# Gate and up products as seven products of halves per feature tile, and a down projection in three chunks whose input is read back from DRAM

## The chip, the cores and the metric

The kernel runs on one core of one Trainium2 chip. The metric is the device time of one execution in microseconds (us), from the first instruction to the last. The core has five engines with a queue of instructions each: TensorE (PE in the profile; PEld are its weight loads), VectorE (DVE), ScalarE (ACT), GpSimd (POOL) and SyncE (SP), which here issues the DMA transfers. Each engine works through its own queue in order, and waits on semaphores for the others.

## The reference

One hybrid decoder layer with batch 1, 512 tokens, 2048 features and 5632 hidden features in the channel sub-layer, all in float32.

```
mod = silu(c) @ w_ada + b_ada
sh_m, sc_m, g_m, sh_f, sc_f, g_f = split(mod, 6)
h = modulate(rms_norm(x, norm_mix_g), sh_m, sc_m)
p = h @ w_in
...                      # RG-LRU heads and RWKV-7 heads over all tokens
x = x + g_m * (concat([y_a, y_b]) @ w_out)
h = modulate(rms_norm(x, norm_ffn_g), sh_f, sc_f)
gate, up = split(h @ w_gu, 2)
x = x + g_f * ((silu(gate) * up) @ w_down)
return rms_norm(x, final_norm_g)
```

Here `modulate(h, shift, scale)` is `h * (1 + scale) + shift`. The change is about the last three lines.

## The kernel before

**Layout.** Activations lie transposed: 128 features on the partitions, all 512 tokens along the free axis. A tile of features is one index `k` (16 tiles of the 2048 features) or `f` (44 tiles of the 5632 hidden ones). Weights are packed ahead of the launch so that one DMA brings the 128 output columns of one tile for a run of input features.

**Products.** A float32 product is made of three products in the format float32r. `split_into` (L105, L106) splits an operand exactly: ACT casts it to the high part, and DVE subtracts that part from the operand to get the low one. `mm3` (L124 to L126) then multiplies high by high, high by low and low by high. `load_split` issues the DMA of a weight piece into a raw tile (L115) and splits it, ahead of what else is queued on ACT and DVE if its data are there (`high_priority`). `gemm_steps` runs a whole product over its input tiles `k`; each step is three matmuls of 128x512, each with a weight load of its own.

**Order.** A scheduler takes the program in the order in which it is written and puts each instruction on its engine's queue; `high_priority` moves work ahead. In the mixing sub-layer `weave` orders several streams by estimated latencies; that part is left as it is. A tile pool has a fixed number of buffers per tag, and a new tile waits until the buffer's last reader is done.

**The channel sub-layer** is `channel` (L912 to L977). First the second half of the output projection (`project`) adds to the residual tiles `x1`, which stay in SBUF, and modulation columns 68 to 79 are made beside it (`mod_steps`, L198 and L199). Then comes the norm (`norm`), and `modulate` (L247, L251, L252) makes 16 pairs of high and low parts, `hhi` and `hlo`. Four chunks follow. Each chunk makes 11 hidden tiles: for each, a gate product and an up product of 16 steps of `k`, silu (L957), a product (L958) and a split into `shi` and `slo`, which stay in SBUF. Then the chunk multiplies its 11 tiles into all 16 output tiles and adds the result to `x1` (L969). The last modulation columns, 80 to 95, are made in the first chunk (L963 to L965). At the end come a norm and the stores of the output.

The raw weight tiles of this part hold 1024 columns (8 input tiles) and have two buffers, the split ones three (L939). The SBUF pool `big` has 32 buffers of one 128x512 tile. PSUM has eight banks under five tags, `mm` 2, `st` 1, `gr` 2, `ch` 2 and `y` 1; here `mm`, `st` and `gr` take turns.

## Time and profile before

| | |
|---|---|
| time, three runs | 2515.35, 2515.86 (median) and 2519.14 us |
| profiled execution, span | 2515.8 us, 30983 instructions; no other time is given for it |
| up to 914 us | mixing sub-layer and the first half of the output projection, PE busy 849.5 us |
| 914 to 1045 us | second half of the output projection and the norm, PE busy 120.2 of 131 us |
| 1045 to 2495 us | gate, up and down, PE busy 1440.8 of 1450 us, DVE 500.5, ACT 348.1, POOL none |
| 2495 to 2516 us | last norm and stores, PE busy 3.4 us |
| DMA | 333.22 MB in all, mean 132 GB/s |

A matmul's row in the profile is longer than the time until the next one starts, since matmuls overlap in the engine. A busy PE is thus read by counting matmuls over a stretch of time, not by the length of a row. In the lists of instruction groups, a line has the source line, the engine, the operation, output and inputs by the program's names, shapes and the count; then busy time and mean duration of one in ns; then the idle time ahead of them with what ended it. In a timeline, the first number is the start in us, and the second the duration.

### The profile page before, as it was taken

Reading aid. Unit: us, or ns where it says so; the run is one execution under the profiler, and the core shown is the slowest. Engines: PE = TensorE matmul, PEld = TensorE weight load, DVE = VectorE, ACT = ScalarE, POOL = GpSimd, SP = SyncE. Lnnn points to the kernel's source line nnn. Section 1 sums busy time; section 2 is a strip of 40 time slices with the busy share of each in tenths; the row PEclk is TensorE's granted clock in tenths of the full one; section 3 lists DMA queues with packets and bytes.
Section 4 is the critical chain, followed back from the end, with each engine's and each line's share of the span. In section 5 each row is a group of like instructions: output and inputs, shape, how many; then the busy total and the mean of one; then the engine's idle time right before and its main releaser. Section 6 shows DMA issues by size and latency. Waiting matters only on the chain.

```text
span 2515.8 us, 30983 instructions
## 1 busy us (share of the span) xinstructions
PE 2413.9 (96%) x11560; PEld 1953.4 (78%) x11560; DVE 1380.4 (55%) x3111; ACT 843.7 (34%) x1340; POOL 82.0 (3%) x131
## 2 busy tenths in 40 slices
PE   5999999999999999899999999999999999999997
PEld 3677777877777886687788888888888888888885
DVE  7979898999969847854423322233322233222244
ACT  4357364455355333432222222222222222222221
POOL 0000111111101000000000000000000000000000
PEclk9999998999999999999999999999999999999998
DMA  8864444444342438366423332323333233333233
GB/s 304 308 219 130 148 128 143 131 152 144 125 135 81 143 108 283 119 195 194 160 90 95 108 100 93 101 83 98 106 98 99 89 92 105 101 93 100 85 95 112
DMA packets 138938, 333.22 MB, mean 132 GB/s; under 512 B 15458, under 2 KB 28898, under 8 KB 134690
## 3 DMA queue, kind: packets, MB, share of 16 engines
q1 hardware_dynamic: 138788, 331.25, 40.7%
q8 instruction: 90, 1.47, 0.2%
q14 instruction: 60, 0.49, 0.1%
HBM read 322.92 MB, written 7.87 MB: 131 GB/s over the span
## 4 chain that ended last, share of the span: by engine, by line
PE 72%; DVE 9%; DMA 7%; issue 1%; ACT 1%; SPq 0%; POOL 0%; DVEq 0%; ACTq 0%
PE ps_mm L124 10%; PE ps_mm L126 10%; PE ps_mm L125 10%; PE ps_gr L126 6%; PE ps_st L124 6%; PE ps_gr L124 6%; PE ps_st L126 6%; PE ps_gr L125 6%; PE ps_st L125 6%; DMA adaq<-in_w_ada 6%; DVE adaq L199 2%; DVE wlo L106 2%; DVE rw_xp L764 1%; DVE rw_x L766 1%; DMA wraw<-in_w_out 1%
## 5 line engine op out<-in xcount | busy, mean ns | idle before, releaser
L106 DVE TENSOR_TENSOR wlo<-wraw,whi 128x1024 fp32r<-128x1024 f32 (+2 forms) x552 | 496.7, 902 | 730.2 <-ACT whi L105 721.1
L105 ACT CAST whi<-wraw 128x1024 fp32r<-128x1024 f32 (+2 forms) x552 | 436.6, 792 | 1292.4 <-PE ps_mm L125 401.1
L124 PE MATMUL ps_mm<-hhi,whi 128*128 128x512 f32 x1020 | 417.1, 410 | 9.8 <-ACT hhi L251 7.2
L126 PE MATMUL ps_mm<-hhi,wlo 128*128 128x512 f32 x1020 | 407.2, 399 | 1.7 <-DVE wlo L106 1.6
L125 PE MATMUL ps_mm<-hlo,whi 128*128 128x512 f32 x1020 | 406.5, 399 | 0.8 <-DVE hlo L252 0.7
L124 PEld LDWEIGHTS ps_mm<-hhi,whi 128*128 128x128 f32 x1020 | 193.4, 190 | 53.2 <-ACT hhi L251 9.9
L125 PEld LDWEIGHTS ps_mm<-hlo,whi 128*128 128x128 f32 x1020 | 193.7, 190 | 43.4 <-DVE hlo L252 4.8
L126 PEld LDWEIGHTS ps_mm<-hhi,wlo 128*128 128x128 f32 x1020 | 193.8, 190 | 42.3 <-DVE wlo L106 3.0
L199 DVE SCALAR_TENSOR_TENSOR adaq<-adaq,cbq 128x512 f32<-128x512 f32 x256 | 173.5, 687 | 92.9 <-DMA adaq<-in_w_ada 85.1
L126 PE MATMUL ps_gr<-hhi,wlo 128*128 128x512 f32 x496 | 193.7, 390 | 3.1 <-DVE wlo L106 3.1
L126 PE MATMUL ps_st<-hhi,wlo 128*128 128x512 f32 x496 | 193.6, 390 | 2.0 <-DVE wlo L106 2.0
L124 PE MATMUL ps_st<-hhi,whi 128*128 128x512 f32 x496 | 194.0, 391 | 1.6 <-ACT hhi L251 1.6
L125 PE MATMUL ps_gr<-hlo,whi 128*128 128x512 f32 x496 | 193.5, 390 | 0.0
L125 PE MATMUL ps_st<-hlo,whi 128*128 128x512 f32 x496 | 193.5, 390 | 0.0
L124 PE MATMUL ps_gr<-hhi,whi 128*128 128x512 f32 x496 | 192.6, 391 | 0.0
L126 PEld LDWEIGHTS ps_gr<-hhi,wlo 128*128 128x128 f32 x496 | 93.4, 188 | 23.6 <-DVE wlo L106 4.1
L126 PEld LDWEIGHTS ps_st<-hhi,wlo 128*128 128x128 f32 x496 | 93.4, 188 | 21.8 <-DVE wlo L106 2.5
L124 PEld LDWEIGHTS ps_st<-hhi,whi 128*128 128x128 f32 x496 | 93.5, 188 | 21.6 <-ACT hhi L251 2.2
L125 PEld LDWEIGHTS ps_gr<-hlo,whi 128*128 128x128 f32 x496 | 93.7, 189 | 19.6
L124 PEld LDWEIGHTS ps_gr<-hhi,whi 128*128 128x128 f32 x496 | 93.7, 189 | 19.4
L125 PEld LDWEIGHTS ps_st<-hlo,whi 128*128 128x128 f32 x496 | 93.3, 188 | 19.8 <-DVE hlo L252 0.3
L766 DVE TENSOR_TENSOR rw_x<-rw_x,rw_xp 128x27 f32<-128x27 f32 (+23 forms) x496 | 94.7, 196 | 5.7
(312 smaller groups left out, 3809.6 us busy)
## 6 DMA issues: line engine op xcount, KB each, us to landing
wraw<-in_w_gu SPq DMA_DIRECT2D x176, 512.0 KB, 3.6
adaq<-in_w_ada SPq DMA_DIRECT2D x256, 256.0 KB, 3.3
wraw<-in_w_in SPq DMA_DIRECT2D x160, 256.0 KB, 3.0
ada<-in_w_ada SPq DMA_DIRECT2D x32, 1024.0 KB, 7.2
wraw<-in_w_down SPq DMA_DIRECT2D x64, 512.0 KB, 3.5
wraw<-in_w_out SPq DMA_DIRECT2D x64, 256.0 KB, 3.3
wraw<-in_w_down SPq DMA_DIRECT2D x64, 192.0 KB, 2.3
x<-in_x SPq DMA_DIRECT2D x32, 256.0 KB, 5.3
```

The source lines that it names most:

```text
L105: nc.scalar.copy(out=hi, in_=src)
L106: nc.vector.tensor_tensor(out=lo, in0=src, in1=hi.bitcast(F32), op=ALU.subtract)
L124: mm(ps, lhsT=w[0], rhs=x[0], start=start, stop=False)
L125: mm(ps, lhsT=w[0], rhs=x[1], start=False, stop=False)
L126: self.pe = mm(ps, lhsT=w[1], rhs=x[0], start=False, stop=stop).ins
L199: nc.vector.scalar_tensor_tensor(out=t, in0=t, scalar=1.0, in1=cb, op0=ALU.mult, op1=ALU.mult, accum_out=part[:, m, h:h + 1])
L764: tt(out=pr[:, :n, :j], in0=at[:, s + 1:, s:s + 1].to_broadcast([P, n, j]), in1=x[:, s:s + 1, :j].to_broadcast([P, n, j]), op=ALU.mult)
L766: tt(out=x[:, s + 1:, :j], in0=x[:, s + 1:, :j], in1=pr[:, :n, :j], op=ALU.add)
```

## The change

The product of a gate tile and an up tile with the hidden input is now taken as a two by two block product. The tokens are halved (256 each), the input features are halved (1024 each), and the two columns of blocks are the gate tile and the up tile. Of the eight block products that this takes, the form of Strassen and Winograd needs seven, on sums and differences of blocks. `b11` and `b21` are the two halves of a gate tile's weights, `b12` and `b22` those of the up tile's.

`group` makes one gate tile and one up tile by seven products, in the order 1, 2, 6, 5, 7, 4, 3. Each has 8 steps of `k` with three matmuls of 128x256, into half a PSUM bank. The weight sums are made on the raw tiles ahead of their split: `b11 + b12` on POOL (L1139), plus `b22` on DVE into `t2` (L1141), `t2 + b21` on DVE (L1144) and `b12 + b22` on POOL (L1152). DVE takes the seven products out of PSUM (L1136 to L1162) and ACT one (L1133). `gu_end` (L1010) applies silu, multiplies and stores the hidden tile to DRAM.

The activations' side of each product is made once, by `operands` and `from_h`: it modulates halves of `x1` in place (L970, L972), POOL makes sums and differences of them (L994 to L996, L1007), and each is split into a tile `comb`. This is done beside the first two groups, which run in step; the other 42 follow one by one. The residual is stored to DRAM beforehand (`x1d`, L944), because `x1` is overwritten, and read again (`x1r`, L1046).

The down projection starts when all 44 hidden tiles are there. It has three chunks, of 15, 15 and 14 tiles, which are read from DRAM into `sraw` (two buffers) and split. A chunk's product for one output tile takes a piece of 1024 columns and one of 896 or 768. The 64 steps for the modulation columns 80 to 95 stand in groups 10 onward in the program, two a group; in DVE's queue they come in groups 2 to 12 (L199). The pool `big` has 8 buffers of four tiles (`quad_view`). The weight pool `wf` has ten raw buffers instead of two; it is opened at the start of `channel`, and its tiles of 1024 columns serve the second half of the output projection as well.

```diff
-        self.open_weights(ctx, "wf", 1024, 2, 3)
+        self.wmctx.close()
+        self.open_weights(ctx, "wf", 1024, 10, 3)
...
+            def done(m):
+                self.square(acc, xt[m], m, fp)
+                nc.sync.dma_start(out=self.x1d[m], in_=xt[m])
+            self.after_project = done
...
-        h = [self.modulate(xt[k], self.cols[:, 16 + k:17 + k], rstd, self.mod[:, 48 + k:49 + k],
-                           yp.tile([P, S], F32R, tag="h", name="hlo")) for k in range(KT)]
...
-                pg, pu = ps(), ps()
-                self.gemm(pg, i["w_gu"][2 * m], h)
-                self.gemm(pu, i["w_gu"][2 * m + 1], h)
-                t = fp.tile([P, S], F32, tag="ft", name="sil", bufs=2)
-                hi = fp.tile([P, S], F32R, tag="shi", name="shi", bufs=FC)
-                lo = fp.tile([P, S], F32R, tag="slo", name="slo", bufs=FC)
-                self.split_into(hi, lo, t)
-                s.append((hi, lo))
-            if cf == 0:
-                with self.tc.issue_after(last):
-                    self.mod_cols(range(80, 96), self.wm, ("raw", 3, "raw", 3))
...
-                self.gemm(p, i["w_down"][cf, m], s)
...
+        self.cp = gctx.enter_context(tc.tile_pool(name="cp", bufs=6))
+        self.ev = gctx.enter_context(tc.tile_pool(name="ev", bufs=2))
...
+        def modulate(q, side):
+            sl = slice(side * 256, side * 256 + 256)
+            for z in range(4):
+                k = 4 * q + z
+                v = quads[q][:, z, sl]
+                stt(out=v, in0=v, scalar=self.cols[:, 16 + k:17 + k], in1=rstd[:, sl],
+                    op0=ALU.mult, op1=ALU.mult)
+                nc.scalar.activation(out=v, in_=v, func=AF.Identity, bias=self.mod[:, 48 + k:49 + k])
...
+        def from_h(p):
+            if p == 1:
+                modulate(0, 0)
+                modulate(1, 0)
+                return [view(0, 0), view(1, 0)]
+            if p == 2:
+                modulate(2, 0)
+                modulate(3, 0)
+                return [view(2, 0), view(3, 0)]
+            if p == 6:
+                for j in range(2):
+                    modulate(j, 1)
+                    modulate(2 + j, 1)
+                    t = self.staging()
+                    pool_tt(out=t, in0=view(j, 1), in1=view(2 + j, 1), op=ALU.subtract)
+                    pool_tt(out=view(j, 1), in0=view(j, 0), in1=view(j, 1), op=ALU.subtract)
+                    pool_tt(out=view(j, 0), in0=t, in1=view(j, 0), op=ALU.subtract)
+                    s1.append(t)
+                return [view(0, 0), view(1, 0)]
+            if p == 5:
+                return s1
+            if p == 7:
+                return [view(0, 1), view(1, 1)]
+            if p == 4:
+                return [view(2, 1), view(3, 1)]
+            s4 = [self.staging(), self.staging()]
+            for j in range(2):
+                pool_tt(out=s4[j], in0=view(2 + j, 0), in1=view(j, 0), op=ALU.add)
+            return s4
+        def gu_end(m, g, u):
+            nc.scalar.activation(out=g, in_=g, func=AF.Silu)
+            nc.vector.tensor_tensor(out=g, in0=g, in1=u, op=ALU.mult)
+            nc.sync.dma_start(out=sd[m], in_=g)
...
+        mods = self.mod_steps(range(80, 96), fq, ("ft", 2, "x1", 2))
+        g0, g1 = self.group(stage, 0), self.group(stage, 1)
+        for p in order[:-1]:
+            self.operands(stage, p)
+            next(g0)
+            next(g1)
+        self.operands(stage, 3)
+        for g in (g0, g1):
+            for _ in g:
+                pass
+        for m in range(2, FT):
+            g = self.group(stage, m)
+            for p in order:
+                next(g, 0)
+                if m >= 10 and p in (6, 4):
+                    next(mods, 0)
...
+        xt = []
+        for k in range(KT):
+            xt.append(self.quad_view(k, "x1r", F32))
+            nc.sync.dma_start(out=xt[k], in_=self.x1d[k])
+        gctx.close()
+        for n in (15, 15, 14):
+            s = []
+            for f in range(base, base + n):
+                t = fq.tile([P, S], F32, tag="x1", name="sraw", bufs=2)
+                nc.sync.dma_start(out=t, in_=sd[f])
+                hi = sp.tile([P, S], F32R, tag="shi", name="shi", bufs=15)
+                lo = sp.tile([P, S], F32R, tag="slo", name="slo", bufs=15)
+                self.split_into(hi, lo, t)
+                s.append((hi, lo))
+            for m in range(KT):
+                p = self.ps(("mm", "gr", "ch")[m % 3])
+                self.gemm(p, i["w_down"][m][:, base * P:(base + n) * P], s)
+                stt(out=xt[m], in0=p, scalar=self.mod[:, 80 + m:81 + m], in1=xt[m], op0=ALU.mult, op1=ALU.add)
...
+    def staging(self):
+        t = self.wp.tile([P, self.wc], F32, tag="raw", name="stage", bufs=self.wb[0])
+        return t.rearrange("p (k n) -> p k n", n=256)
...
+    def operands(self, stage, p):
+        at = {1: 0, 2: 2, 6: 4, 5: 6, 7: 8, 4: 10, 3: 12}[p]
+        out = []
+        for j, src in enumerate(stage["get"](p)):
+            if 4 <= at + j < 10:
+                t = self.cp.tile([P, 4, S], F32R, tag="c", name="comb")
+            else:
+                t = self.big.tile([P, 4, S], F32R, tag="h", name="comb")
+            n = src.shape[1]
+            t = t.rearrange("p k n -> p (k n)").rearrange("p (h k n) -> p h k n", h=2, n=256)
+            self.split_into(t[:, 0, :n], t[:, 1, :n], src)
+            out.append(t)
+        stage["ops"][p] = out
...
+        raw = []
+        for src in stage["src"](m):
+            t = self.wp.tile([P, self.wc], F32, tag="raw", name="wraw", bufs=self.wb[0])[:, :N]
+            raw.append(t)
+        for z in (0, 2, 1, 3):
+            nc.sync.dma_start(out=raw[z], in_=stage["src"](m)[z])
+        b11, b12, b21, b22 = raw
+        def product(tag, p, w):
+            with tc.high_priority():
+                hi = self.wp.tile([P, self.wc], F32R, tag="whi", name="whi", bufs=self.wb[1])
+                lo = self.wp.tile([P, self.wc], F32R, tag="wlo", name="wlo", bufs=self.wb[1])
+                self.split_into(hi[:, :N], lo[:, :N], w)
+            ops = stage["ops"][p]
+            ps = self.ps(tag)[:, :256]
+            for k in range(n):
+                sl = slice(k * P, k * P + P)
+                o = ops[k // 4]
+                self.mm3(ps, (hi[:, sl], lo[:, sl]), (o[:, 0, k % 4], o[:, 1, k % 4]), k == 0, k == n - 1)
+            return ps
+        def tmp(tag):
+            return self.ev.tile([P, 256], F32, tag=tag, name="ev_" + tag, bufs=1)
+        g = self.ev.tile([P, S], F32, tag="g", name="ev_g")
+        u = self.ev.tile([P, S], F32, tag="u", name="ev_u")
+        ps = product("mm", 1, b11)
+        a = tmp("a")
+        nc.scalar.copy(out=a, in_=ps)
+        yield
+        ps = product("gr", 2, b21)
+        tt(out=g[:, :256], in0=ps, in1=a, op=ALU.add)
+        yield
+        with tc.high_priority():
+            pool_tt(out=b11, in0=b11, in1=b12, op=ALU.add)
+            t2 = self.wp.tile([P, self.wc], F32, tag="t2", name="t2", bufs=1)[:, :N]
+            tt(out=t2, in0=b11, in1=b22, op=ALU.add)
+        ps = product("ch", 6, t2)
+        with tc.high_priority():
+            tt(out=b21, in0=t2, in1=b21, op=ALU.add)
+        b = tmp("b")
+        tt(out=b, in0=ps, in1=a, op=ALU.add)
+        yield
+        p5 = product(("st", "y")[par], 5, b11)
+        tt(out=u[:, :256], in0=p5, in1=b, op=ALU.subtract)
+        yield
+        with tc.high_priority():
+            pool_tt(out=b12, in0=b12, in1=b22, op=ALU.add)
+        ps = product("mm", 7, b12)
+        c = tmp("c")
+        tt(out=c, in0=ps, in1=b, op=ALU.add)
+        tt(out=u[:, 256:], in0=p5, in1=c, op=ALU.subtract)
+        yield
+        ps = product("gr", 4, b21)
+        tt(out=g[:, 256:], in0=ps, in1=c, op=ALU.add)
+        yield
+        ps = product("ch", 3, b22)
+        tt(out=u[:, :256], in0=ps, in1=u[:, :256], op=ALU.add)
+        stage["end"](m, g, u)
...
-    wd = a["w_down"][0]
-    o["w_down"] = np.stack([_tiles(wd[c * 1408:(c + 1) * 1408]) for c in range(4)])
+    o["w_down"] = _tiles(a["w_down"][0])
```

The order of instructions on three engines shows where this puts the work. In all rows the name of a line is followed by the operation, the output, the inputs and the shape; a number behind x counts equal rows in a row.

On DVE, in the middle of the gate and up products, before: L106 makes the low part of a piece of weights (`wlo`) or of a hidden tile (`slo`), L958 multiplies silu of the gate by the up product.

```order
L106 TENSOR_TENSOR wlo<-wraw,whi 128x1024 x4
L958 TENSOR_TENSOR sil<-sil,ps_mm 128x512
L106 TENSOR_TENSOR wlo<-wraw,whi 128x1024
L106 TENSOR_TENSOR slo<-sil,shi 128x512
L106 TENSOR_TENSOR wlo<-wraw,whi 128x1024 x3
L958 TENSOR_TENSOR sil<-sil,ps_gr 128x512
```

On DVE at the same place now, the most of one group: L1155 to L1162 take products out of PSUM, L1141 and L1144 add weights, and `t` with a number is the tile `t2`.

```order
L1155 TENSOR_TENSOR ev_c<-ps_mm,ev_b 128x256
L1156 TENSOR_TENSOR ev_u<-ps_st,ev_c 128x256
L106 TENSOR_TENSOR wlo<-wraw,whi 128x1024
L1159 TENSOR_TENSOR ev_g<-ps_gr,ev_c 128x256
L1141 TENSOR_TENSOR t_14527<-wraw 128x1024
L106 TENSOR_TENSOR wlo<-wraw,whi 128x1024
L1144 TENSOR_TENSOR wraw<-t_14527,wraw 128x1024
L106 TENSOR_TENSOR wlo<-t_14527,whi 128x1024
L1162 TENSOR_TENSOR ev_u<-ps_ch,ev_u 128x256
L1012 TENSOR_TENSOR ev_g<-ev_g,ev_u 128x512
```

Between the splits stand sums that need POOL's result: L1141 of the next group reads what L1139 wrote, and it stands ahead of the split of the second product's weights and ahead of this group's last eviction, L1162.

On POOL at the start of the channel sub-layer now (before, POOL has nothing from here to the end). `x1_8166` to `x1_8169` are the four quads of `x1`, `stage` are tiles of the weight pool.

```order
L994 TENSOR_TENSOR stage_10550<-x1_8166,x1_8168 128x1024
L995 TENSOR_TENSOR x1_8166<-x1_8166 128x4x256
L996 TENSOR_TENSOR x1_8166<-stage_10550,x1_8166 128x4x256
L994 TENSOR_TENSOR stage_10570<-x1_8167,x1_8169 128x1024
L1007 TENSOR_TENSOR stage_10854<-x1_8168,x1_8166 128x1024
L995 TENSOR_TENSOR x1_8167<-x1_8167 128x4x256
L996 TENSOR_TENSOR x1_8167<-stage_10570,x1_8167 128x4x256
L1007 TENSOR_TENSOR stage_10855<-x1_8169,x1_8167 128x1024
```

All eight are new. The second operand of product 6 (`x1_8167` after the last L996) stands behind six of them, and behind the four weight sums of the first two groups, which stand ahead of these rows. Afterwards POOL alternates between L1139 and L1152, one of each a group.

On SP, where gate and up give way to the down projection, before (at the end of the first chunk): L198 loads the weights of the modulation columns, L115 pieces of weights.

```order
L115 DMA wraw<-in_w_gu 128x1024
L198 DMA adaq<-in_w_ada 128x512 x2
L115 DMA wraw<-in_w_gu 128x1024 x11
L115 DMA wraw<-in_w_down 128x1024
L115 DMA wraw<-in_w_down 128x384
```

On SP at that passage now: L1013 stores the last hidden tile, L1054 reads hidden tiles back.

```order
L115 DMA wraw<-in_w_down 128x1024
L115 DMA wraw<-in_w_down 128x896
L115 DMA wraw<-in_w_down 128x1024
L1013 DMA s_10347<-ev_g 128x512
L115 DMA wraw<-in_w_down 128x896
L115 DMA wraw<-in_w_down 128x1024
L1054 DMA sraw<-s_10306 128x512
L1054 DMA sraw<-s_10307 128x512
L1054 DMA sraw<-s_10308 128x512
```

The first pieces of `w_down` go out ahead of the last store; the reads of the hidden tiles from the third on stand behind it (the first two were issued earlier), and each of them waits for one of the two buffers.

More of the change, by code (lines that the diff above doesn't have):

```diff
@@ L241, in norm, with quad_view, modulate @@
         return ps
-    def modulate(self, x, col, rstd, sh, lo=None):
+    def quad_view(self, k, name, dtype):
+        if k % 4 == 0:
+            self.quad[name] = self.big.tile([P, 4, S], dtype, tag="h", name=name)
+        return self.quad[name][:, k % 4]
+    def modulate(self, k, x, col, rstd, sh):
         nc = self.nc
@@ L400, in filler @@
             self.ya = [self.load_y(k, self.big) for k in range(8)]
-            self.x1 = [self.big.tile([P, S], F32, tag="h", name="x1") for k in range(KT)]
+            self.x1, self.x1q = [], []
+            for k in range(KT):
+                self.x1.append(self.quad_view(k, "x1", F32))
+                if k % 4 == 0:
+                    self.x1q.append(self.quad["x1"])
             for k in range(KT):
@@ new lines, in group @@
+    def group(self, stage, m):
+        nc, tc = self.nc, self.tc
+        tt, pool_tt = nc.vector.tensor_tensor, nc.gpsimd.tensor_tensor
+        n = stage["n"]
+        N = n * P
+        par = self.ngroup % 2
+        self.ngroup += 1
+        raw = []
[54 more added lines that the diff above has]
+        stage["end"](m, g, u)
```

94 lines of the change are left out of this document (50 added, 44 removed).

## The prediction

> **What bounds the kernel now.** I read the page first, then the busy time by stretches, then the engines' timelines at three places.
>
> ```profile
> PE 2413.9 (96%) x11560; PEld 1953.4 (78%) x11560; DVE 1380.4 (55%) x3111; ACT 843.7 (34%) x1340; POOL 82.0 (3%) x131
> PE 72%; DVE 9%; DMA 7%; issue 1%; ACT 1%; SPq 0%; POOL 0%; DVEq 0%; ACTq 0%
> 1000.00:1100.00 100.00, 93.28 (x399) 74.55 (x398) 75.94 (x155) 39.62 (x55) 0.00 (x0) 0.97 0.47 154
> 1100.00:1200.00 100.00, 95.92 (x421) 78.32 (x420) 49.38 (x104) 21.21 (x25) 0.00 (x0) 1.00 0.62 196
> 1200.00:1300.00 100.00, 97.39 (x429) 79.90 (x428) 37.48 (x56) 24.61 (x29) 0.00 (x0) 1.00 0.39 126
> 1400.00:1600.00 200.00, 200.00 (x884) 165.61 (x883) 58.96 (x58) 48.09 (x55) 0.00 (x0) 1.00 0.31 99
> ```
>
> PE is busy 96% and carries 72% of the chain that ended last. The stretches (columns: PE, PEld, DVE, ACT, POOL, clock, DMA share, GB/s) say more: from 1400 on PE starts 884 matmuls in 200 us, one per 0.2263 us, with no idle time, at granted clock 1.00; DVE, ACT and DMA stand at a third or less. So in the channel sub-layer a matmul's slot on PE is the price, and its count the lever. The 4224 matmuls of gate and up cost 955.9 us and the 2112 of the down projection 477.9.
>
> ```profile
> 1046.04 0.80 PE L124 MATMUL ps_st<-hhi,whi 128*128 128x512 f32 x1 [1.59 <-ACT hhi L251]
> 1046.63 0.63 PE L124 MATMUL ps_gr<-hhi,whi 128*128 128x512 f32 x1
> ...
> 1049.62 0.63 PE L126 MATMUL ps_gr<-hhi,wlo 128*128 128x512 f32 x1
> L969 DVE SCALAR_TENSOR_TENSOR x<-ps_gr,mod,x x22: 750/751/751, 1305.3 to 2494.6; 128x512 f32<-128x512 f32 x22
> ```
>
> These products run from 1046.0 to the last eviction at 2494.6: 1448.6 us, so only 14.8 of it is not matmul slots. Behind 2494.6 stand 21.2 us of norm and stores to the span's end, 2515.8, which is 0.06 under the median of the three runs; I sum against the span and carry the result over as it is.
>
> **The slot of a 256-column matmul** decides most, and before has none in this form. Gate and up become 44 groups of 7 products of 8 feature tiles by three matmuls: 7392 at half the columns. Break-even is 955.9 / 7392 = 0.1293 us. I bound the slot by three rows.
>
> ```profile
> 415.50 0.97 PEld L643 LDWEIGHTS ps_gr<-rw_ar,bd_k 128*128 128x128 f32 x8
> ...
> 416.39 0.19 PEld L124 LDWEIGHTS ps_mm<-hhi,whi 128*128 128x128 f32 x1
> 704.24 0.40 PE L125 MATMUL ps_mm<-hlo,whi 128*128 128x512 f32 x1
> ...
> 705.87 0.40 PE L126 MATMUL ps_mm<-hhi,wlo 128*128 128x512 f32 x1
> ```
>
> First, each matmul has its own weight load. A load is 0.19 long, but eight of L643 start within 0.89 us: loads overlap and follow each other at 0.111, so a slot under 0.111 is out, and the load's 0.19 is no bound. Second, a slot has a part that isn't columns: just after the norm, with PE at a lower clock (0.97 over that stretch), seven matmuls take 2.99 us, 0.427 each; that is twice 0.2136, against the slot of 0.2263. Some 0.0127 thus shows only at full clock. If it goes with the columns, the slot is half of 0.2263, 0.1131; if each matmul pays it, 0.1068 + 0.0127 = 0.1195. Third, in the crowded mixing stage seven matmuls take 1.63 us (0.2329), a surcharge of 0.0193, which gives 0.1261 at most. I take 0.1195: load and stream both fill the slot nearly, so nothing is left to hide a fixed part. A group is then 168 x 0.1195 = 20.08 us against 96 x 0.2263 = 21.72.
>
> **What the other engines must do in these 20 us.**
>
> ```profile
> L106 DVE TENSOR_TENSOR wlo<-wraw,whi 128x1024 fp32r<-128x1024 f32 x237 | 290.1, 1225 | 450.0 <-ACT whi L105 444.1
> L105 ACT CAST whi<-wraw 128x1024 fp32r<-128x1024 f32 x237 | 249.6, 1054 | 782.8 <-PE ps_gr L125 196.7 <-PE ps_st L125 196.1 <-PE ps_mm L125 191.8
> L106 DVE TENSOR_TENSOR slo<-sil,shi 128x512 fp32r<-128x512 f32 x44 | 30.1, 684 | 0.0
> L611 DVE TENSOR_TENSOR rw_ar<-rw_pb,mix_r x16: 412/418/422, 199.9 to 848.1; 128x256 f32<-128x256 f32 x16
> L199 DVE SCALAR_TENSOR_TENSOR adaq<-adaq,cbq 128x512 f32<-128x512 f32 x64 | 43.7, 691 | 73.1 <-DMA adaq<-in_w_ada 72.6
> L616 POOL TENSOR_SCALAR bd_a<-rw_ar x32: 844/990/1830, 213.4 to 849.4; 64x256 f32<-64x256 f32 x32
> L775 POOL TENSOR_SCALAR bd_xt<-rw_xs x64: 517/527/1017, 275.1 to 885.0; 32x128 f32<-32x128 f32 x64
> L490 POOL MEMSET bd_bt<- x2: 522/522/522, 187.1 to 187.6; 128x512 f32 x2
> ```
>
> DVE has seven splits and two sums of 1024 columns (9 x 1.225), seven evictions of 256 (0.418 each) and a product of 512 (0.69): 14.6 us. ACT has seven casts of 1.054 and about one more: 8.4. Both fit. POOL gets two additions of 1024 columns, and before has none on it. From L775 to L616 128 elements cost 0.327 us at the shortest, 2.55 ns each; carried on to 1024 that is 2.8 us, which I take, since these rows read and write as the addition does. The lower end is the memset's 1.02 ns an element, 1.05 us; the upper is the mean of the two longest-delayed L616 below, 2.97 / 2 = 1.49 for 256, the same factor of 1.76 over 0.844: 4.9 us.
>
> The additions do not only fit or not, they stand in a ring. Weights of the next group's first product are cast (1.05) and split (1.23) once the buffer of product 7 comes free; POOL may then overwrite them with b11 + b12; DVE adds b22 (1.23) and only behind that, by its order, splits the weights of product 2 (1.23), which PE needs before products 2, 6, 5 and 7, 96 matmuls. With some 0.3 for hand-overs (POOL starts 0.08 after its releaser, below) the ring is 5.0 + x + 11.5, x POOL's addition. With 2.8 it is 19.3, under PE's 20.08: hidden, with 0.8 to spare. Past x = 3.6 each us more costs 42 us.
>
> **Getting started.** Before, PE waited 1.59 us for the first operand and then ran along. Now operands for seven products are made, with two groups in step. DVE reads the norm at 1044.5.
>
> ```profile
> L247 DVE SCALAR_TENSOR_TENSOR modt<-x,cols,ps_ch x16: 740/743/748, 1044.5 to 1069.2; 128x512 f32<-128x512 f32 x16
> ```
>
> A half of L247 (0.743 less 0.27, half the difference of the 1024 and 512 splits) is 0.47. Until the upper half of the third quad is modulated DVE does 24 of these (11.3), eight splits (9.8), two sums (2.5), an eviction (0.4) and waits some 2 us for buffers that PE frees: 26. Then seven POOL operations in a row (19.6) stand before the second operand of product 6, its cast and split take 2.3, and DVE's queue behind them has 14 splits and eight evictions (20.6) until the last operand of product 3; PE ends 4.3 later. That is 73 us, I say 74; POOL's bounds make it 62 to 89. Two groups alone are 40, so 34 us are lost here.
>
> **Down projection.** Its 2112 matmuls stay at 0.2263. What changes is the supply: 44 tiles come back from DRAM through two buffers, and SP issues the third of them behind the last group's store, which stands behind DVE's last product.
>
> ```profile
> wraw<-in_w_gu SPq DMA_DIRECT2D x176, 512.0 KB, 3.6
> yraw<-y SPq DMA_DIRECT2D x14, 256.0 KB, 2.8
> L105 ACT CAST shi<-sil 128x512 fp32r<-128x512 f32 x44 | 27.0, 614 | 31.6 <-DVE sil L958 31.6
> ```
>
> A pair of tiles takes 2.8 to land, 0.61 and 0.68 to split and about 0.2 of hand-overs: 4.3 us. The first chunk's 15th tile is ready some 3.3 + 6.5 x 4.3 = 31 us after the last gate product; PE interleaves two output tiles and eight features of a third by then, 36 x 3 x 0.2263 = 24.4. I take 10 us with the restart (bounds 0 and 31). At the two other chunk ends tiles come while the last output tile still runs (10.2 us), so 4 each (0 to 14). The same eviction count goes from four chunks to three, on an idle DVE: nothing.
>
> **Smaller terms.** The 64 L199 of the last modulation columns now run in groups 2 to 12, six a group on DVE (4.1 us; 18.8 of 20.08 in all). Before, they held PE back too: the stretches 1100 to 1300 lack 34 of 884 matmuls, 7.7 us. I take 5 (0 to 30, if each group lost a whole L199 wait). In the output projection 4 MB of extra stores share the queue where L199's loads already crowd it, and the wider weight buffers open only when the mixing pools close: 3, between -8 (before's weight waits there gone) and 10. Weight traffic of 2 MB a group is as before, at 99 GB/s.
>
> **Sum.** 1044.5 + 74 + 42 x 20.08 (843.4) + 5 + 10 + 477.9 + 8 + 21.2 + 3 = 2487.0, against 2515.8: 28.8 less. The products win 70 us; the start and the chunks give back more than half.
>
> **The rivals.**
>
> *The slot is shorter.* If the 0.0127 goes with the columns, or L643's 0.111 is all, a group is 19.0 or 18.65 and the end 2442 or 2427; the ring (16.1 or so with 2.8) still hides. For it: the surcharge vanished at the lower clock, as a feed limit would. Against: two limits this close rarely both hold. Chance 0.15, at 2435. The Trainium skill, "TensorE: Matmul & The Clock Gate", Back-to-back issue gap, gives columns at 2.4 GHz plus 2.5 ns when warm, 0.109 here; by that the sum would be 2413, but it gives 0.216 for 512, and the row says 0.2263.
>
> *The ring sets the pace, and the kernel is slower.* The place is the wait of L1141 for POOL in every group; it decides from x = 3.6, and past 4.3 the whole gain is gone.
>
> ```profile
> 213.39 2.97 POOL L616 TENSOR_SCALAR bd_a<-rw_ar 64x256 f32<-64x256 f32 x2 [23.34 <-DVE rw_ar L609]
> 212.89 0.42 DVE L609 SCALAR_TENSOR_TENSOR rw_ar<-rw_pb,rw_kk 128x256 f32<-128x256 f32 x1
> 213.83 0.69 DVE L590 TENSOR_TENSOR rw_a<-rw_a,rw_kk 128x512 f32<-128x512 f32 x1
> 214.43 0.89 DVE L584 SCALAR_TENSOR_TENSOR rw_t<-mix_r,vecs,mix_k 128x512 f32<-128x512 f32 x1
> ```
>
> Where DVE runs beside it, POOL's two L616 take 2.97 instead of 1.69, and DVE's L584 0.89 where a neighbour of its size takes 0.69. At 4.9 the ring is 21.4, the end 2542. Or POOL's second addition, issued at once behind the first, holds L1141 up for its whole length: 5.0 + 5.6 + 11.5 = 22.1, the end 2572. Against it: in the ring DVE mostly waits while POOL adds, so there is little to collide with, and L590 kept its 0.69. Chance 0.20, at 2545. The Trainium skill, "SBUF — State Buffer", Who interferes with whom, says that a DVE instruction with two SBUF inputs and a GpSimd one that reads SBUF exclude each other for the whole instruction. By that the second case holds; the trace bears it out in part, since POOL was held up by 1.28 us, but DVE only by 0.2.
>
> *The losses eat the gain.* Start, chunks and modulation at their upper ends together add some 28 us: 2515, no change. Chance 0.07. *The slot reaches 0.1261*: a group is 21.2, 2534, chance 0.05.
>
> **Chances.** The forecast, 2455 to 2510 with 2487 the likeliest, has 0.53. The range takes in the short slot and the ring: 2430 to 2555. Faster by over 0.2%, about what a measurement of this kernel can tell from no change (under 2510.8): 0.53 + 0.15 and little else, 0.69. Within it 0.08. Slower 0.23.
>
> **What would show it.** Steady stretches at 8.4 matmuls a us with PE never idle prove the slot, 8.8 the shorter one. PE idle before product 2, released by DVE's `wlo` and this by POOL, proves the ring. The first two groups should end near 1118, with PE idle until POOL's seventh operation; the down projection should show one gap of about 10 us and two small ones. I am wrong if the 256-column slot is over 0.129, or if POOL's additions take over 4.3 us.

## The result, and the profile after

| | before | changed |
|---|---|---|
| median of four runs each | 2515.61 us (2508.80 to 2519.14) | 2591.61 us (2586.90 to 2603.59) |
| ratio, 95% interval | | 1.0321 (1.0303 to 1.0339): slower |
| span of the profiled execution | 2515.8 us | 2584.7 us |

The forecast was 2487 us, faster. The first and fourth parts of the page of the changed kernel (busy time by engine, and the chain that ended last by engine) answer to the two lines with which the prediction began.

```profile
PE 2377.2 (92%) x14728; PEld 2067.3 (80%) x14728; DVE 1851.2 (72%) x3588; ACT 1004.3 (39%) x1497; POOL 359.8 (14%) x227
PE 31%; issue 27%; DVE 11%; POOL 10%; DMA 10%; ACT 1%; SPq 0%; POOLq 0%; DVEq 0%; ACTq 0%
```

PE's busy time fell by 37 us and the time rose by 69. POOL, at 0% of the chain before, now carries 10% of it. The busy time by stretches (columns as before: PE, PEld, DVE, ACT, POOL, clock, DMA share, GB/s) says where:

```profile
1000.00:1100.00 100.00, 72.45 (x333) 60.03 (x332) 78.16 (x153) 36.84 (x56) 11.76 (x4) 0.86 0.63 204
1100.00:1200.00 100.00, 76.59 (x574) 74.96 (x575) 79.37 (x110) 42.01 (x51) 34.79 (x13) 0.85 0.47 150
1200.00:1300.00 100.00, 86.44 (x660) 85.22 (x659) 82.01 (x125) 31.51 (x35) 22.24 (x9) 0.91 0.53 172
1400.00:1600.00 200.00, 195.57 (x1613) 193.75 (x1613) 155.78 (x167) 77.50 (x85) 52.64 (x18) 1.00 0.36 117
2200.00:2400.00 200.00, 198.53 (x870) 162.30 (x869) 69.08 (x74) 48.45 (x56) 0.00 (x0) 1.00 0.38 114
```

At full clock PE starts 1613 matmuls of 256 columns in 200 us, 0.124 each, with 4.4 us of idle time. Between 1000 and 1300 it is idle a fifth of the time. The trace gives the stages by their first and last matmul; against the prediction's sum:

| stage | predicted | changed | off by |
|---|---|---|---|
| until DVE reads the norm (L970) | 1047.5 (1044.5 + 3) | 1076.8 | +29.3 |
| from there to the third group | 74 | 74.3 | +0.3 |
| 42 groups | 848.4 (843.4 + 5) | 913.1 | +64.7 |
| from the last gate product to the last of the down projection | 495.9 (10 + 477.9 + 8) | 499.5 | +3.6 |
| norm and stores | 21.2 | 20.9 | -0.3 |
| span | 2487.0 | 2584.7 | +97.7 |

Two stages hold nearly all of it, and the 42 groups fall in two kinds: the first nine, with the modulation steps beside them, take 24.8 us on average (21.2 to 28.6), the other 33 take 20.91 each, to 0.02. What happens in one of the 33 is seen in the timelines of DVE, POOL and PE around 1500 us (first number the start, second the duration):

```profile
1495.16 1.23 DVE L106 TENSOR_TENSOR wlo<-wraw,whi 128x1024 fp32r<-128x1024 f32 x1
1497.08 0.42 DVE L1159 TENSOR_TENSOR ev_g<-ps_gr,ev_c 128x256 f32<-128x256 f32 x1 [0.69 <-PE ps_gr L126]
1498.91 1.23 DVE L1141 TENSOR_TENSOR t<-wraw 128x1024 f32<-128x1024 f32 x1 [1.40 <-POOL wraw L1139]
1500.05 3.43 DVE L106 TENSOR_TENSOR wlo<-wraw,whi 128x1024 fp32r<-128x1024 f32 x1
```

```profile
1496.47 2.40 POOL L1139 TENSOR_TENSOR wraw<-wraw 128x1024 f32<-128x1024 f32 x1 [14.98 <-DVE wlo L106]
1498.95 3.44 POOL L1152 TENSOR_TENSOR wraw<-wraw 128x1024 f32<-128x1024 f32 x1
```

```profile
1502.52 0.28 PE L126 MATMUL ps_mm<-comb,wlo 128*128 128x256 f32 x1
1502.64 0.28 PE L124 MATMUL ps_gr<-comb,whi 128*128 128x256 f32 x1
1502.76 0.28 PE L125 MATMUL ps_gr<-comb,whi 128*128 128x256 f32 x1
1503.53 0.39 PE L126 MATMUL ps_gr<-comb,wlo 128*128 128x256 f32 x1 [0.49 <-DVE wlo L106]
```

The matmuls follow each other at 0.120. The split of product 1 ends at 1496.39; POOL adds; DVE adds (L1141); and then the split of product 2, 1.23 us of work, takes 3.43: it ends 1.1 after POOL's second sum (1498.95 + 3.44 = 1502.39), so it did its work only from about there on. PE waits for it. From that matmul on to the point at which product 7 gives its weight buffer free are 11.5 us, and the ring closes: cast 1.05 + split 1.23 + 2.40 + 1.14 (start of L1141 to start of the split) + 3.43 + 11.5 + hand-overs of 0.15 = 20.9, the measured group. PE's own 168 x 0.120 = 20.16 no longer sets the pace.

In the first nine groups the same ring has more in it, as DVE's timeline near 1275 us shows:

```profile
1273.24 0.69 DVE L199 SCALAR_TENSOR_TENSOR adaq<-adaq,cbq 128x512 f32<-128x512 f32 x1 [2.00 <-DMA adaq<-in_w_ada]
1273.86 0.08 DVE L199 DVE_READ_ACCUMULATOR adaq<-adaq,cbq 128x1 f32 x1
1273.86 1.22 DVE L106 TENSOR_TENSOR wlo<-wraw,whi 128x1024 fp32r<-128x1024 f32 x1
1274.99 0.69 DVE L199 SCALAR_TENSOR_TENSOR adaq<-adaq,cbq 128x512 f32<-128x512 f32 x1
...
1277.98 1.23 DVE L1141 TENSOR_TENSOR t<-wraw 128x1024 f32<-128x1024 f32 x1 [1.95 <-POOL wraw L1139]
1279.12 3.37 DVE L106 TENSOR_TENSOR wlo<-wraw,whi 128x1024 fp32r<-128x1024 f32 x1
```

The split that lets POOL start (1273.86) stood 2.00 us behind an L199 that waited for its DMA. Over the nine groups DVE stood 25.6 us ahead of 57 such products, and PE was idle for 27.0 of 223 us. After its longer waits PE then went on at half clock, as PE's timeline behind the split of 1279.12 shows, and the stretch from 1283 on (granted clock 0.50):

```profile
1282.55 0.58 PE L126 MATMUL ps_gr<-comb,wlo 128*128 128x256 f32 x1 [4.29 <-DVE wlo L106]
1282.93 0.42 PE L124 MATMUL ps_gr<-comb,whi 128*128 128x256 f32 x1
1283.14 0.41 PE L125 MATMUL ps_gr<-comb,whi 128*128 128x256 f32 x1
```

```profile
1283.00:1288.00 5.00, 5.00 (x25) 5.00 (x25) 5.00 (x9) 0.52 (x1) 0.00 (x0) 0.50 0.24 81
```

The matmuls follow each other at 0.21 there, not 0.120. In the nine groups 123 of them came 0.17 to 0.40 behind the one before; against 0.120 each that makes some 12 us.

### The profile page after: what moved, and what is told of

It reads as the page before. It is cut to its first block, busy times and chain, and to the rows that moved or that the text cites. A ratio compares the mean times of both kernels' runs of the same rounds, so it can differ in the third digit from the quotient of the medians.

```text
span 2584.7 us, 38502 instructions
## 1 busy us (share of the span) xinstructions
PE 2377.2 (92%) x14728; PEld 2067.3 (80%) x14728; DVE 1851.2 (72%) x3588; ACT 1004.3 (39%) x1497; POOL 359.8 (14%) x227
## 4 chain that ended last, share of the span: by engine, by line
PE 31%; issue 27%; DVE 11%; POOL 10%; DMA 10%; ACT 1%; SPq 0%; POOLq 0%; DVEq 0%; ACTq 0%
POOL wraw L1152 5%; PE ps_mm L124 5%; PE ps_mm L125 5%; PE ps_mm L126 5%; DMA adaq<-in_w_ada 5%; POOL wraw L1139 4%; DVE wlo L106 2%; PE ps_ch L126 2%; PE ps_ch L125 2%; PE ps_ch L124 2%; DVE adaq L199 2%; PE ps_gr L124 2%; PE ps_gr L125 2%; PE ps_gr L126 2%; DMA sraw<-s 2%
## 5 line engine op out<-in xcount | busy, mean ns | idle before, releaser
L105 ACT CAST whi<-wraw 128x1024 fp32r<-128x1024 f32 (+3 forms) x591 | 518.3, 879 | 1035.3 <-PE ps_mm L125 359.9
L106 DVE TENSOR_TENSOR wlo<-wraw,whi 128x1024 fp32r<-128x1024 f32 (+3 forms) x591 | 684.6, 1160 | 247.4 <-ACT whi L105 237.7
L126 PE MATMUL ps_gr<-comb,wlo 128*128 128x256 f32 x704 | 208.9, 297 | 39.8 <-DVE wlo L106 39.8
L199 DVE SCALAR_TENSOR_TENSOR adaq<-adaq,cbq 128x512 f32<-128x512 f32 x256 | 183.7, 725 | 62.9 <-DMA adaq<-in_w_ada 55.0
L126 PE MATMUL ps_mm<-hhi,wlo 128*128 128x512 f32 x556 | 225.8, 406 | 0.0
L1139 POOL TENSOR_TENSOR wraw<-wraw 128x1024 f32<-128x1024 f32 x44 | 107.7, 2448 | 830.9 <-DVE wlo L106 634.5
L124 PE MATMUL ps_ch<-comb,whi 128*128 128x256 f32 x704 | 201.6, 287 | 21.4 <-ACT comb L105 21.4
L124 PE MATMUL ps_mm<-comb,whi 128*128 128x256 f32 x704 | 200.8, 285 | 3.6 <-ACT comb L105 3.6
L126 PE MATMUL ps_mm<-comb,wlo 128*128 128x256 f32 x704 | 201.2, 286 | 3.1 <-DVE wlo L106 3.1
L124 PE MATMUL ps_gr<-comb,whi 128*128 128x256 f32 x704 | 203.6, 289 | 0.0
L125 PE MATMUL ps_gr<-comb,whi 128*128 128x256 f32 x704 | 203.6, 289 | 0.0
L125 PE MATMUL ps_ch<-comb,whi 128*128 128x256 f32 x704 | 201.8, 287 | 0.5 <-DVE comb L106 0.5
L126 PE MATMUL ps_ch<-comb,wlo 128*128 128x256 f32 x704 | 201.5, 286 | 0.3 <-DVE wlo L106 0.3
L125 PE MATMUL ps_mm<-comb,whi 128*128 128x256 f32 x704 | 200.7, 285 | 0.5 <-DVE comb L106 0.5
L1152 POOL TENSOR_TENSOR wraw<-wraw 128x1024 f32<-128x1024 f32 x44 | 148.9, 3384 | 3.5
```

Of the source, the lines that this page charges most:

```text
L105: nc.scalar.copy(out=hi, in_=src)
L106: nc.vector.tensor_tensor(out=lo, in0=src, in1=hi.bitcast(F32), op=ALU.subtract)
L124: mm(ps, lhsT=w[0], rhs=x[0], start=start, stop=False)
L125: mm(ps, lhsT=w[0], rhs=x[1], start=False, stop=False)
L126: self.pe = mm(ps, lhsT=w[1], rhs=x[0], start=False, stop=stop).ins
L199: nc.vector.scalar_tensor_tensor(out=t, in0=t, scalar=1.0, in1=cb, op0=ALU.mult, op1=ALU.mult, accum_out=part[:, m, h:h + 1])
```

## The experiments

Each is the changed kernel with one edit, unless it says otherwise. Spans are those of the profiled execution, to be compared with 2584.7. Most of these kernels were executed once, and four executions of the changed kernel had spans from 2584.7 to 2601.4; the argument therefore rests on stages and rows of the traces more than on spans.

**Both weight sums on DVE.**

```diff
-            pool_tt(out=b11, in0=b11, in1=b12, op=ALU.add)
+            tt(out=b11, in0=b11, in1=b12, op=ALU.add)
...
-            pool_tt(out=b12, in0=b12, in1=b22, op=ALU.add)
+            tt(out=b12, in0=b12, in1=b22, op=ALU.add)
```

> Both weight sums of a group (b11 + b12, b12 + b22) run on DVE instead of POOL. Theory A (the ring: DVE's split for product 2 stands behind POOL's first sum and then is shut out for the length of POOL's second one): the ring shortens from 20.9 to about 18.7 us, PE's 168 x 0.120 = 20.16 sets the pace, steady groups take 20.2 us instead of 20.91, and no split of 1024 columns takes 3.4 us any more; 33 steady groups give back 25 us, the groups with modulation columns also a part, the span is 2540 to 2560 (2584.7 in the changed kernel). Theory B (DVE's total work is the limit, POOL only shows it): DVE gets 2.4 us more a group, and groups take 21.5 us or more, the span 2600 or more.

Span 2532.5. The stretch from 1400 on:

```profile
1400.00:1600.00 200.00, 200.00 (x1669) 200.00 (x1668) 162.94 (x194) 82.14 (x90) 0.00 (x0) 1.00 0.39 122
```

1669 matmuls in 200 us, none of it idle: 0.120 each, groups of 20.16. DVE is busier than in the changed kernel (162.94 of 200 us against 155.78), and PE does not wait for it. Theory A holds, B falls. The gain is larger than expected, since the groups with modulation steps fell too: the first nine take 21.2 on average, and all 42 together 11.9 us over 20.16 each. Yet DVE stood as long ahead of their L199 as in the changed kernel. The two rows are DVE's groups of L199 in the stretch of the early groups, in the changed kernel (1151 to 1374 us) and here (1154 to 1410 us):

```profile
L199 DVE SCALAR_TENSOR_TENSOR adaq<-adaq,cbq 128x512 f32<-128x512 f32 x57 | 41.7, 734 | 25.6 <-DMA adaq<-in_w_ada 25.2
L199 DVE SCALAR_TENSOR_TENSOR adaq<-adaq,cbq 128x512 f32<-128x512 f32 x57 | 39.1, 687 | 25.8 <-DMA adaq<-in_w_ada 25.6
```

The granted clock between 1155 and 1400 was 1.00. So the waits alone are not the price; they cost much where the ring has no slack.

**Only the second sum on DVE.**

```diff
-            pool_tt(out=b12, in0=b12, in1=b22, op=ALU.add)
+            tt(out=b12, in0=b12, in1=b22, op=ALU.add)
```

> Only the second weight sum (b12 + b22) runs on DVE; the first stays on POOL, in place. Theory A (the split of product 2's weights is shut out for the length of POOL's second sum, 2.2 us of it in the ring): the ring falls from 20.9 to 19 or 19.8, steady groups take 20.2 us, no split takes 3.4 us. Theory A1 (POOL's first sum in the ring is what costs, 2.45 us): steady groups stay at 20.7 us or more.

Span 2549.6, steady groups 20.16. DVE's timeline in a group, from 1700 us on:

```profile
1703.69 1.23 DVE L1152 TENSOR_TENSOR wraw<-wraw 128x1024 f32<-128x1024 f32 x1 [1.47 <-POOL wraw L1139]
1704.83 1.22 DVE L1141 TENSOR_TENSOR t<-wraw 128x1024 f32<-128x1024 f32 x1
1705.97 1.22 DVE L106 TENSOR_TENSOR wlo<-wraw,whi 128x1024 fp32r<-128x1024 f32 x1
```

The split takes 1.22 again, with POOL's first sum still in the ring. A1 falls: without the shut-out by the second sum the ring stays under PE's time, so that shut-out is what puts it over.

**Both sums on POOL, the first out of the ring.**

```diff
-            pool_tt(out=b11, in0=b11, in1=b12, op=ALU.add)
+            pool_tt(out=b12, in0=b11, in1=b12, op=ALU.add)
...
-            pool_tt(out=b12, in0=b12, in1=b22, op=ALU.add)
+            pool_tt(out=b11, in0=t2, in1=b11, op=ALU.subtract)
```

Products 5 and 7 and L1141 read the other tile accordingly.

> The two POOL sums stay on POOL, but the first writes over b12 instead of b11 and the second is t2 - b11 (the same sum): the first no longer waits for the split of product 1. Theory A: the ring without POOL's first sum is under 20 us, steady groups take 20.2 us, the span falls by 20 to 30 us. Theory A2 (it is not the ring but the mutual shut-out of DVE and POOL alone, 5.8 us a group wherever POOL's sums stand): steady groups stay at 20.7 to 21, the span within 10 us of 2584.7.

Span 2551.4, steady groups 20.16, as theory A has it. POOL's rows show that collisions remain:

```profile
1699.52 3.36 POOL L1139 TENSOR_TENSOR wraw<-wraw 128x1024 f32<-128x1024 f32 x1 [10.76 <-DVE ev_b L1146]
1706.52 2.40 POOL L1152 TENSOR_TENSOR wraw<-t,wraw 128x1024 f32<-128x1024 f32 x1 [3.64 <-DVE wlo L106]
```

POOL is still held up by DVE (3.36), and DVE by POOL, though less than before: beside these two sums splits of 1.23 take 1.69 and 1.97, not 3.43. Nothing that PE waits for stands behind them. A2 falls as it was put: collisions outside the ring cost nothing here. Either sum taken out of the ring frees all of the 0.75 us, because the ring was over PE's time by no more.

**Modulation steps two a group.**

```diff
                 if m >= 10 and p in (6, 4):
-                    next(mods, 0)
+                    with tc.issue_after(self.ev_ins):
+                        next(mods, 0)
```

`ev_ins` is the group's last eviction so far, L1146 or L1159.

> The 64 modulation steps are tied to DVE's evictions of the group in which they are written, two a group in groups 10 to 41 instead of six in groups 2 to 10. Theory C (the products of these steps wait for their DMA at the head of DVE's queue, ahead of the splits of the ring, and cost 4 us a group): groups 2 to 9 fall from 24.8 us to 20.9, the groups from 10 on rise by less than 0.5 each, the span is 2545 to 2565. Theory D (these groups are slow because the stream of weights is not yet ahead): they stay above 23 us, and the span at 2575 to 2585.

Span 2550.3. All 42 groups take 20.9 us, the early ones and those that now have two steps. The stretch from 1200 on, to be compared with the changed kernel's above:

```profile
1200.00:1300.00 100.00, 98.02 (x811) 97.21 (x810) 76.85 (x82) 39.16 (x43) 28.95 (x10) 1.00 0.37 119
```

C holds, D falls: in the changed kernel six to eight L199 a group cost 35 us, with their DMA waits and the low clock behind them; two a group cost nothing.

**x piece by piece**, and **the coarser buffers alone**. The first edit issues one load of x with each output tile of the first half of the output projection. The second is the kernel before with `big` as 8 buffers of four tiles, and nothing else.

```diff
-            for k in range(KT):
-                nc.sync.dma_start(out=self.x1[k], in_=i["x"][:, k])
...
+                    with self.tc.issue_after(self.wdma):
+                        for k in ((0, 1) if m == 0 else (m + 1,)):
```

> The 16 loads of x for the residual are issued one by one among the pieces of w_out in the first half of the output projection, instead of all 16 behind one piece. Theory E (PE's wait of 8.5 us at 822 us is for pieces of w_out that stand behind 4 MB of x in the queue): the wait is under 2 us, everything behind it comes 8 to 11 us earlier, the span is 2573 to 2577. Rival (the later wait at 946 us, for the weight pool, takes the gain up): that wait grows by as much, and the span stays at 2582 to 2586.

> The kernel before with one part of the change alone: the activation pool has 8 buffers of four tiles instead of 32 of one. Theory E2 (the coarser buffers alone move the loads of x ahead of all but one piece of w_out, and PE stands some 8 us at 822 us for it): the wait is there, and the span is 8 to 12 us over the kernel before, a ratio of 1.003 to 1.005. Theory Q (they also make the mixing stage ahead of it later): the fourth chunk of the seventh pair is reached at 818 us or later, and the ratio is 1.006 to 1.009. Rival (the wait is taken up by slack behind it, since the heads' chain is not the end of the stage): ratio under 1.002.

SP's timeline of the kernel before, SP's of the changed kernel, and PE's of quads_only:

```profile
811.26 7.74 SPq L115 DMA_DIRECT2D wraw<-in_w_out  x5
819.05 9.80 SPq L403 DMA_DIRECT2D x<-in_x  x16
```

```profile
813.61 0.33 SPq L115 DMA_DIRECT2D wraw<-in_w_out  x1
813.99 10.20 SPq L412 DMA_DIRECT2D x<-in_x  x16
824.59 13.16 SPq L115 DMA_DIRECT2D wraw<-in_w_out  x7
```

```profile
819.53 0.40 PE L126 MATMUL ps_mm<-yhi,wlo 128*128 128x512 f32 x1
827.53 0.80 PE L124 MATMUL ps_mm<-yhi,whi 128*128 128x512 f32 x1 [7.60 <-ACT whi L105]
```

Before the change five pieces of w_out stood ahead of the 16 loads of x, now one. quads_only has the wait, and a ratio of 1.0053 (1.0034 to 1.0072): E2 holds, and it is this one part of the change, the buffers of four tiles, that does it. It reached the fourth chunk of the seventh pair of heads at 815.2 us, so Q falls. In x_late the wait is gone, and from that chunk to the first matmul of the norm it takes 244.9 us instead of 254.1. The span, 2583.5, is that of the rival all the same, but not for the rival's reason: the wait at 946 us did not grow (7.10 us, 7.43 in the changed kernel). This execution had come to that chunk late, at 827.5 us against 817.8.

**The kernel before once more.**

> The kernel before, unchanged, to see how far its mixing stage moves from one execution to the next: in the kernels run so far, the same instructions reached the fourth chunk of the seventh pair of heads between 2.6 and 12.3 us later than in the first profile of the kernel before. If that is chance, this run shows it anywhere from 815 to 827 us; if the change moves it (the buffers of four tiles), it stays within 2 us of 815.

It came to that chunk at 811.8 us, earlier than either reading had it; span 2510.6. The kernels with the whole change came at 817.8 to 827.5 (eleven profiles, 822.3 on average), the three without it at 811.8 to 815.2 (814.0). The queues stand in the same order up to about there. The change thus seems to cost some 8 us in this stage, with a spread as large; nothing here shows why, and it stays open.

**The rest of what comes ahead of gate and up.** x as above; the first half of the output projection is drained before the old weight pool closes; and eleven buffers instead of four for the modulation weights.

```diff
+        for _ in self.filler:
+            pass
         self.wmctx.close()
...
-            mods = self.mod_steps(range(64 + 4, 80), fp, ("ft", 2, "ad", 4))
+            mods = self.mod_steps(range(64 + 4, 80), fp, ("ft", 2, "ad", 11))
```

> Ahead of the gate and up products only: x loaded piece by piece as in x_late, the rest of the first half of the output projection issued before the old weight pool is closed, and eleven buffers instead of four for the modulation weights beside the second half. Theory F (PE's waits at 946 us and 1031 us are for pieces of w_out: the first because the wide weight pool opens only when the mixing pools close, the second because SP stands at modulation loads that wait for one of four buffers): from the last product of the heads' output (L756 in the changed kernel) to the first modulation of x1 (L970) it takes 115 to 122 us instead of 134.9, and the span is 2555 to 2575. Rival (the stores of x1 crowd the queue whatever the order): 130 us or more.

From the last L756 to the first modulation it took 132.9 us: the rival's number, so F falls for this edit. The span, 2572.4, lies in F's range, but the gain was made ahead of that stage, where the x loads were (last L756 at 934.0 us instead of 942.4). The wait at 1031 us became many of 1 to 2 us, and the one at 943 stayed. In the stretch from 1017 to 1045 the DMA share was 0.88 at 301 GB/s, against 0.41 at 139 in the kernel before; 4 MB of stores and the first weights of gate and up are new there. That fits a full queue, but the stores were not taken out alone.

**Operand sums on DVE.**

```diff
-        pool_tt = nc.gpsimd.tensor_tensor
+        pool_tt = nc.vector.tensor_tensor
         s1 = []
```

> The eight sums and differences of activation blocks run on DVE instead of POOL. Theory G (the start is long because of POOL's chain of seven of them, 20.5 us, with DVE's L199 shut out beside it): from the first L970 to the start of the third group it takes 60 to 68 us instead of 74.3, and the span is 2570 to 2580. Rival (DVE's own queue of splits is the longer chain, and has these eight on top): 74 to 82 us.

68.3 us to the third group instead of 74.3, at the edge of what G expects. The span, 2585.0, is not shorter, where G expected 2570 to 2580: the first ten groups took 3.7 us more, with the modulation steps still in them, and this execution reached the fourth chunk of the seventh pair 3.9 later.

**All of it together**, and **with the hidden tiles read ahead**. The second allots the first chunk's 15 hidden tiles from `big`, ahead of the residual; the tiles of the later chunks come from `big` too, instead of the two buffers.

```diff
+        raws = []
+        for f in range(15):
+            raws.append(self.quad_view(f, "sraw", F32))
+            nc.sync.dma_start(out=raws[f], in_=sd[f])
         xt = []
```

> All edits that took time off together: weight sums and activation sums on DVE, modulation steps two a group, x piece by piece, the old weight pool for the first half, eleven modulation buffers. If the parts add up (start of gate and up at 1050 to 1060, 60 to 68 us for the first two groups, 42 groups of 20.2 us, then as in the changed kernel 500 + 21 us) the span is 2478 to 2500, 0.5 to 1.5% under the kernel before. If DVE is full with the sums and two modulation products a group, groups 10 to 41 take 21 us or more, and it is no faster than before.

> As combo, and the hidden tiles of the first chunk of the down projection are read back into the buffers that the first products' operands leave, 15 at a time, ahead of the residual. Theory H (the down projection lost 21.6 us against its 2112 slots because tiles came through two buffers): it takes 484 to 490 us from the last gate product to its own last matmul instead of 499.5, so 10 to 15 us less than combo. Rival (PE's lower clock after any pause costs most of it): within 4 us of combo.

combo: span 2491.1, ratio to the kernel before 0.9952 (0.9937 to 0.9968). All 42 groups take 20.16, with the sums and two modulation steps on DVE; the third group starts 64.2 us after the first modulation. combo_read: span 2486.3, ratio 0.9892 (0.9867 to 0.9917): 1.1% under the kernel before, and each of its runs under each of combo's. Its down projection takes 485.8 us instead of 498.1, as H says. Its stretches, in gate and up and from the start of the down projection:

```profile
1400.00:1600.00 200.00, 200.00 (x1669) 200.00 (x1668) 172.26 (x229) 81.10 (x88) 0.00 (x0) 1.00 0.45 145
1990.00:2190.00 200.00, 200.00 (x884) 165.57 (x883) 72.34 (x80) 49.81 (x59) 0.00 (x0) 1.00 0.47 147
```

**The wide weight pool opened late** (combo_read, with the pool opened behind the output projection).

```diff
-        self.wmctx.close()
-        self.open_weights(ctx, "wf", 1024, 10, 3)
...
             for _ in mods:
                 pass
+        self.wmctx.close()
+        self.open_weights(ctx, "wf", 1024, 10, 3)
```

> As combo_read, but both halves of the output projection use the old weight pool of 512 columns, and the wide pool opens behind them. Theory F (PE's wait of 7 to 8 us at 946 us and the low clock after it come from the wide pool, which opens only when the mixing pools close): the wait is gone, from the last L756 product to the norm it takes 111 to 114 us as before the change instead of 120 to 130, and if the weights of the first groups still come in time (2 MB, 8 us, while the norm runs) the span is 6 to 12 us under combo_read, 2470 to 2478. Rival (the first groups then wait for their weights): within 4 us of combo_read.

Span 2492.5, ratio 0.9941 (0.9923 to 0.9959). The wait at 946 us is gone, so it did come from the pool. But from the last L756 to the norm it took 120.2 us, 125.4 in combo_read, and not the 111 to 114 expected; and what was won there was more than lost behind it, by the rival's mechanism, as PE's timeline shows:

```profile
1069.11 0.58 PE L124 MATMUL ps_mm<-comb,whi 128*128 128x256 f32 x1 [4.76 <-ACT comb L105]
1070.63 0.58 PE L124 MATMUL ps_mm<-comb,whi 128*128 128x256 f32 x1 [0.94 <-ACT whi L105]
1079.02 0.58 PE L125 MATMUL ps_mm<-comb,whi 128*128 128x256 f32 x1 [7.81 <-DVE comb L106]
```

The weights now come all at once; in these 7.81 us DVE mostly sums and splits weights, ahead of the operand that PE needs. The third group starts 74.3 us after the first modulation, not 66.0.

## Why the prediction was wrong

**The slot was right.** I took 0.1195, the rows say 0.120. The part that does not go with the columns is paid by each matmul: 0.2263 at 512 columns and 0.120 at 256 differ by 0.106, which is what 256 columns cost, and leave some 0.014 at either size. The difference of 0.0005 is 3.3 us in 42 groups.

**The step that failed is the ring.** "With 2.8 it is 19.3, under PE's 20.08: hidden, with 0.8 to spare." POOL's first sum was cheaper than that, 2.40, and the threshold of 3.6 was not reached. What the predicted ring lacked is the second sum, which holds up the split of product 2 for 2.2 us. The prediction had this mechanism, as the second half of a rival at 0.20 (there the sum L1141 was to be held up; in the trace L1141 starts 0.04 ahead of POOL and it is the split behind it), and set it aside because "in the ring DVE mostly waits while POOL adds" and an L590 had kept its 0.69. The waiting holds for the first sum only. The Trainium skill, "SBUF — State Buffer", Who interferes with whom, says that whichever of the two issues first keeps the other out for its whole instruction; the rows above agree, in both directions: L106 at 3.43 behind L1152, and L1152 at 3.44 behind L1141 where L1139 takes 2.40. L1159, which reads PSUM, kept its 0.42 beside L1139. Cost: 0.75 us in 33 groups, 24.6 us.

**The modulation steps were mis-sized.** "I take 5 (0 to 30 ...)": the nine groups lost 41.8 us against 20.16 each. The work of six L199 was counted, and that it fits; their waits, 25.6 us in all, stand in DVE's queue ahead of the split on which POOL waits, so they lengthen a ring that had nothing to spare. The low clock after PE's waits, some 12 us of the 41.8, was not in the term at all. Spread out, the steps cost nothing, and with both sums on DVE waits just as long cost 11.9: the loss belongs to the steps and the ring together. With the ring's 24.6 and the slot's 3.3, the 36.8 beyond the 5 make up the 64.7 of the 42 groups.

**The part ahead of the norm was mis-sized.** "3, between -8 (before's weight waits there gone) and 10": it was 32.3 (29.3 + 3), of which 2.6 came ahead of the fourth chunk of the seventh pair. The prediction never looked at SP's queue in the first half of the output projection, though the order of instructions shows there what quads_only measured: 16 loads ahead of four pieces of w_out, some 9 us. The wide pool cost a wait of 7.43 us at 946 us with a dozen matmuls at the lower clock behind it, and another of 8.71 came at 1031, put down here to modulation loads and a full queue, which no run shows apart. PE's timeline of the changed kernel has both:

```profile
954.07 0.80 PE L124 MATMUL ps_mm<-yhi,whi 128*128 128x512 f32 x1 [7.43 <-ACT whi L105]
...
1040.45 0.80 PE L124 MATMUL ps_mm<-yhi,whi 128*128 128x512 f32 x1 [8.71 <-ACT whi L105]
```

And DVE's last sum of squares ahead of the norm, 0.69 of work, was held up beside POOL's first weight sums:

```profile
1068.98 2.82 DVE L223 TENSOR_TENSOR sqacc<-sqacc,sqt 128x512 f32<-128x512 f32 x1
```

PE stood 6.62 us ahead of the norm's first matmul for it, and 2.77 in combo, where POOL has none of these sums.

**Right were** the start, the down projection and the tail, the first in part by luck. The first and the last of POOL's operations that the start waits for, in the changed kernel:

```profile
1100.70 2.36 POOL L994 TENSOR_TENSOR stage<-x,x 128x1024 f32<-128x1024 f32 x1 [29.44 <-ACT x L972]
...
1118.90 2.34 POOL L996 TENSOR_TENSOR x<-stage,x 128x1024 f32<-128x1024 f32 x1
```

They begin 23.9 us after the first modulation (26 reckoned), last 20.5 (19.6), and the third group starts 29.9 behind them (27). The sum came out at 74.3 against 74 because these errors cancel; single POOL operations took 2.34 to 3.00, and the 2.8 reckoned for each is met only because some were held up beside DVE (L995 takes 2.84 here, and 2.34 in mods_spread, where no L199 stands beside it). Ahead of the down projection PE stood still once, and then ran at the lower clock for a while:

```profile
2064.12 0.28 PE L126 MATMUL ps_ch<-comb,wlo 128*128 128x256 f32 x1
2071.15 0.80 PE L124 MATMUL ps_mm<-shi,whi 128*128 128x512 f32 x1 [6.74 <-ACT shi L105]
```

All of it came to 21.6 us over the 477.9 of the matmuls, where 18 were reckoned: some 14 at the start (10 reckoned) and some 6 at the two chunk ends (8). The time fell outside the range because the ring, the modulation steps and the part ahead of the norm all went wrong at once, two of them past the bounds I had set, while the rivals were priced one at a time. The sum was also made against the span as if it were the time; the runs of the changed kernel lie 2.1 to 2.2 us over their spans.

## What to carry to other kernels

Fewer matmul cycles pay only if what feeds them stays under PE's new time in the order in which it is queued: go once round each ring of buffers (cast, split, sums, products), with every instruction and wait that any of its queues holds ahead of a link, and with what two engines do to each other. The longer waits of PE cost more than their length here, since it went on at half clock. Work that is off the path and waits for DMA belongs on a queue where nothing urgent stands behind it, or is spread until its data are there. When buffers change their size or a pool moves, compare the order of SP's queue too: here some nine microseconds came from that alone, far ahead of the stage that was rewritten.

## What the runs showed of the hardware

POOL and DVE kept each other out for whole instructions when both took their operands from SBUF: 1.23 became 3.43 on DVE, 2.40 became 3.44 on POOL, and an L199 of 0.69 took 2.83 to 2.86 three times beside POOL's operand sums, as here in the changed kernel's timeline of DVE:

```profile
1110.98 2.86 DVE L199 SCALAR_TENSOR_TENSOR adaq<-adaq,cbq 128x512 f32<-128x512 f32 x1
```

One of POOL's additions of 128x1024 takes 2.40 alone, twice DVE's 1.22. After idle times of 6.7, 7.4 and 8.7 us in the changed kernel (the rows at 2071.15, 954.07 and 1040.45) PE went on at slots of 0.43 or more for 512 columns, for 5 to 6.5 us, at a granted clock of 0.50. Against slots of 0.2263 each such wait cost some 3 us more than its length. An idle time of 4.29 us at 1282.55 was followed by slots of 0.21 for 256 columns.
